# Decays of a Mamba-2 chunk summed in one product each, and two input panels fed from the same k-tile

## The chip, the cores and the metric

The kernel runs on one core of a Trainium2 chip. The metric is the device time of one execution in microseconds (us); the inputs lie in the chip's memory (HBM) when it starts. Five engines work side by side, each through its own list of instructions in order: TensorE (PE in the profile; PEld is its weight loading), VectorE (DVE), ScalarE (ACT), GpSimd (POOL) and SyncE (SP), which here issues the DMA transfers.

## The reference

One decoder layer on 256 tokens of width 1024, all in float32:

```
proj = rms_norm(x) @ w_in            # q, k, v, z, xBC, dt, two gates
y_a  = moba_attention(q, k, v)       # 16 heads; at 256 tokens: causal attention
y_b  = mamba2_mixer(z, xBC, dt)      # conv, chunked scan, gate, grouped norm
x = x + (sigmoid(g_a)*(y_a@Wa) + sigmoid(g_b)*(y_b@Wb)) @ W_out
x = x + swiglu(rms_norm(x))
x = x + (p @ W_pp) * sigmoid(rms_norm(x) @ W_pg)
```

The change touches the scan. With dt = softplus(dt_raw + bias) and a = -dt exp(a_log) for each token and each of 32 heads, in two chunks of 128 tokens:

```
xdt      = xh * dt
decay_in[l, s] = exp(a[s+1] + ... + a[l])   for l >= s, else 0
y_diag   = (C B^T * decay_in) @ xdt
w_end[s] = exp(a[s+1] + ... + a[127]);  states = B^T (xdt * w_end)
y_off    = C @ state of the chunk before, times exp(a[0] + ... + a[l])
```

## The kernel before

Nearly every product is a 512-column *panel*: two PSUM tiles of 128 tokens x 512 columns (`g`, four banks, so two panels at a time), summed over k-tiles of 128 input features. To keep float32 accuracy, weights and activations are split into a high part in the fast float32r format and a low part (`wh`, `wl`, `ah`, `al`), and each k-tile and token half takes three products: ah wh, ah wl, al wh (`Panel.add`, L280). A k-tile is thus six matmuls of 512 columns, a panel of the input projection 48.

Weights come by DMA two k-tiles at a time (512 KB; tag `raw`, four buffers), ScalarE rounds them to `wh` (three buffers) and VectorE subtracts to get `wl` (six buffers) (`load`, L220). The first panel's first half is loaded by single k-tiles, each k-tile of x (128 KB, `load_x`) beside its weights (256 KB); all vectors of constants (`vecs`, 121 KB, with the norm gain of x in columns 0 to 7) come in one transfer behind the first x tile. `split_h` (L262) scales a k-tile of x by the gain and splits it.

The panels stand in a list (L34): six of xBC first (group 4, then 0, 5, 1, 2, 3), then k, q, z and so on. Behind each panel an evacuation (`evac_*`) reads its PSUM; that of xBC multiplies by `rstd1`, which `x_stats` (L311) makes from a second copy of x (`xk`, two transfers of 512 KB). All smaller work (dt, convolution, scan, attention) is made of Python generators that a `Filler` steps between the matmuls of the panels: `fill.now` adds up the TensorE time of what has been issued, and after each part a generator waits until `fill.now` has grown by an entry of the table `LAG` (ns, L68). This gives the program's order. The framework's planner then orders each engine's list with a timing model of its own, by priority: weights ("w"), evacuations ("ev"), small work ("bg"), main matmuls ("mm"). Main matmuls keep their order among themselves.

The scan: `dt_task` (L336) makes dt and a, and splits a into `a_h` and `a_l`; four small products give the sums for `e0` (w_end of chunk 0) and `e1`. For each unit (group g, half qd: four heads) and each chunk c, `decay_rows` (L538) has GpSimd lay out a_h and a_l as two 128 x 4 x 128 tiles (`rr`, four buffers, first used by x), with entry [s, l] = a[s] where l >= s; `seg` (L576) multiplies each by the strict triangle `gt_r` and adds both in PSUM:

```
mm(pseg, gt_r, rr.pop((g, qd, c, 0)), True, False)
mm(pseg, gt_r, rr.pop((g, qd, c, 1)), False, True)
```

ScalarE takes the exponential, VectorE multiplies by the masked C B^T (`cbm`). `prep` makes `xdt` (times dth = dt/2), `out_` the products with it. There are 8 units, so 16 such pairs. `ssm_out` needs the finished groups: it steps the filler until they are there.

Of the kernel before, what the change touches and what calls it, by code (L numbers as in the profile page):

```python
# [68 lines left out]
    "dt": 8257, "dt.t": 2343, "dt.e": 17162, "dt.end": 5569, "xbc": 3815, "xbc.t": 2321, "xbc.end": 7699,  # L69
    "z": 3815, "z.t": 1286, "z.end": 1943, "qk": 13149, "qk.t": 2429, "qk.end": 663, "v": 2577, "cb": 500,  # L70
    "rows": 3610, "prep": 3559, "seg": 722, "seg.next": 7665, "out": 4912, "out.xdt": 3186, "out.end": 0,
    "off": 5300, "off.end": 0, "finish": 6096, "finish.ones": 9336, "sc": 0, "sc.tr": 3063, "tr": 2317,
    "tr.val": 4578, "val": 3570, "val.end": 7415, "m": 500, "res": 6182, "ff": 5466, "ff.end": 5564,
# [34 lines left out]
def tile_layer(ctx: ExitStack, tc: tile.TileContext, xt, xk, pt, vec, w_dt, w_big, w_dn2, w_pp, out):  # L108
# [19 lines left out]
    def nm(s):  # L128
        uid[0] += 1
        return f"{s}_{uid[0]}"  # L130
# [47 lines left out]
    with prio("w"):  # L178
# [23 lines left out]
        nc.gpsimd.tensor_copy(le_r, m_tmp[:, 2])  # L202
        le_q = const.tile([P, P], F32, name="le_q")
# [7 lines left out]
    v = const.tile([P, V_N], F32, name="vecs")  # L211
    xraw = [sb.tile([P, 2, T], F32, tag="rr", bufs=4, name=nm("xraw")) for _ in range(4)]

    def load_x(k, n):
        nc.sync.dma_start(xraw[k // 2][:, k % 2 : k % 2 + n], xt[:, k : k + n])  # L215

    chunk_no = [0]
    first = []

    def load(src, nk):  # L220

        with prio("w"):
            parts = []
            for k in range(0, nk, 2):
                raw = sb.tile([P, 2, 512], F32, tag="raw", bufs=4, name=nm("raw"))
                wh = sb.tile([P, 2, 512], F32R, tag="wh", bufs=3, name=nm("wh"))
                wl = sb.tile([P, 2, 512], F32R, tag="wl", bufs=6, name=nm("wl"))
                n = 2 if len(first) > 1 else 1
                for j in range(0, 2, n):
                    js = slice(j, j + n)  # L230
                    if not first and k + j:
                        load_x(k + j, 1)
                    nc.sync.dma_start(raw[:, js], src[:, k + j : k + j + n])  # L233
                    if not first and not k + j:
                        load_x(0, 1)
                        nc.sync.dma_start(v, vec)
                    if not first and k + j:
                        split_h(k + j)
                    w_ = act(wh[:, js], raw[:, js])
                    if not first:  # L240
                        tc.keep_in_program_order(w_)
                        if not k + j:
                            split_h(0)
                    nc.vector.tensor_sub(wl[:, js], raw[:, js], wh[:, js].bitcast(F32))  # L244
                parts += [(wh[:, 0], wl[:, 0]), (wh[:, 1], wl[:, 1])]
            first.append(1)
            if len(first) == 1:
                load_x(4, 2)
                load_x(6, 2)
        return parts  # L250
# [11 lines left out]
    def split_h(k):  # L262
        g = v[:, V_G1 + k : V_G1 + k + 1]
        xk_ = xraw[k // 2][:, k % 2]
        tc.keep_in_program_order(act(h_act[k][0], xk_, scale=g))
        stt(h_act[k][1], xk_, g, h_act[k][0].bitcast(F32), op0=ALU.mult, op1=ALU.subtract)

    class Panel:
# [3 lines left out]
        def __init__(self, cut=False):  # L272
            self.ps = [psg.tile([P, 512], F32, tag="g", name=nm("g")) for _ in range(2)]
            self.pieces = [(tt, WHOLE, self.ps[tt]) for tt in range(2)]
            if cut:
                other = pb([512])
                self.pieces[1:] = [(1, HALVES[0], self.ps[1][:, HALVES[0]]), (1, HALVES[1], other[:, HALVES[1]])]
            self.first = True

        def add(self, parts, acts, last):  # L280
            n = len(parts)
            if last:
                runs = [(pc, k) for pc in self.pieces for k in range(n)]
            else:
                runs = [(pc, k + j) for k in range(0, n, 2) for pc in self.pieces for j in range(2)]
            for (tt, c, ps), k in runs:
                ah, al = acts[k]
                wh, wl = parts[k]
                ts = slice(tt * P, tt * P + P)
                with prio("mm"):  # L290
                    mm(ps, ah[:, ts], wh[:, c], self.first and k == 0, False, main=True)
                    mm(ps, ah[:, ts], wl[:, c], False, False, main=True)
                    mm(ps, al[:, ts], wh[:, c], False, last and k == n - 1, main=True)
                fill.step()
            self.first = False
# [6 lines left out]
    parts0 = next_chunk()  # L302
    with prio("w"):
        for k in range(4, 8):
            split_h(k)
# [27 lines left out]
    e1 = const.tile([P, 32], F32, name="e1")  # L333
    done = set()

    def dt_task():  # L336
# [55 lines left out]
        with prio("bg"):  # L392

            pe = pb([2, 32])
            mm(pe[:, 0], gt_r, a_h[:, 0], True, False)
            mm(pe[:, 0], gt_r, a_l[:, 0], False, True)
            mm(pe[:, 1], le_r, a_h[:, 1], True, False)
            mm(pe[:, 1], le_r, a_l[:, 1], False, True)
            act(e0, pe[:, 0], AF.Exp)
            act(e1, pe[:, 1], AF.Exp)  # L400
# [117 lines left out]
    def ssm_task():  # L518
# [57 lines left out]
        def seg(g, qd):  # L576
            for c in range(2):
                with prio("bg"):
                    pseg = pb([4, P])
                    mm(pseg, gt_r, rr.pop((g, qd, c, 0)), True, False)  # L580
                    mm(pseg, gt_r, rr.pop((g, qd, c, 1)), False, True)
# [210 lines left out]
    for n, (kind, i, _) in enumerate(PANELS):  # L792
        if kind == "yb":
            ssm_out(i)
            continue
        pan = Panel()
        for hf in range(2):
            pan.add(parts0 if n == hf == 0 else next_chunk(), h_act[4 * hf : 4 * hf + 4], last=hf == 1)
            if n == 0 and hf == 1:
                x_stats()  # L800
            if n == hf == 0:
                fill.spawn(dt_task(), 0)
        gen = evac[kind](kind, i, pan)
        t = next(gen)
        fill.spawn(gen, 0, t - fill.now)
# [219 lines left out]
```

## Time and profile before

| | us |
|---|---|
| median of 3 runs | 614.92 (614.15 to 614.96) |
| the profiled execution, own time | 614.88 |
| its span in the trace | 613.2 |
| PE busy | 604.2 (99%) |
| VectorE busy | 441.8 (72%) |
| ScalarE busy | 341.5 (56%) |
| GpSimd busy | 60.4 (10%) |
| DMA queue of SyncE | 103.29 MB, 51.8% of 16 DMA engines |

Times in the trace count from the span's start. A matmul's duration is longer than the distance to the next one, because matmuls are pipelined; costs of TensorE are therefore read as distances between starts. A note in square brackets is idle time of that engine before the row, and what ended it.

### The profile page before, as it was taken

The page shows a single profiled execution, that of the slowest core. Times are in us where ns is not written, and L with a number is a line of the kernel's source. Part 1 is how long each engine was busy: PE and PEld are TensorE (multiplying, and loading weights), DVE is VectorE, ACT ScalarE, POOL GpSimd, SP SyncE. Part 2 cuts the span into 40 slices and gives each one's busy share as a digit, 9 for nine tenths or more (in the row PEclk, how much of TensorE's full clock was granted, in tenths as well). Part 3 has the DMA queues.
Part 4 walks back from the last instruction along what each step waited for, and adds up shares of the span by engine and source line. Part 5 has one row for each costly group of instructions (what it writes and reads, how often), then busy time and mean ns, then how long its engine had stood idle before and what let it go on. Part 6 is the DMA issues. An engine that isn't in the chain of part 4 may idle for free.

```text
span 613.2 us, 8146 instructions
## 1 busy us (share of the span) xinstructions
PE 604.2 (99%) x2964; PEld 494.0 (81%) x2964; DVE 441.8 (72%) x712; ACT 341.5 (56%) x522; POOL 60.4 (10%) x61
## 2 busy tenths in 40 slices
PE   7999999999999999999999999999999999999997
PEld 5888888877777878888788888888888888888886
DVE  4489899978898775768897576656676666645465
ACT  5568566646584445568467544656554454435353
POOL 1001206623122200200000000000000000000000
PEclk9999999999999999999999999999999999999999
DMA  8845544344324545554444467555556556565541
GB/s 254 310 160 179 173 149 156 125 161 139 103 93 134 181 142 176 169 178 156 131 155 153 144 190 236 175 183 188 189 165 202 183 171 207 172 196 183 192 151 68
DMA packets 30793, 103.81 MB, mean 169 GB/s; under 512 B 3361, under 2 KB 4385, under 8 KB 30753
## 3 DMA queue, kind: packets, MB, share of 16 engines
q1 hardware_dynamic: 30752, 103.29, 51.8%
q8 instruction: 23, 0.38, 0.2%
q14 instruction: 18, 0.14, 0.1%
HBM read 102.23 MB, written 1.05 MB: 168 GB/s over the span
## 4 chain that ended last, share of the span: by engine, by line
PE 92%; DVE 3%; DMA 1%; POOL 1%; SPq 1%; issue 1%; ACT 0%; POOLq 0%
PE g L164 80%; PE pb L164 7%; PE pb L174 5%; DMA raw<-in_w_big 1%; POOL tiny L479 1%; DVE wl L244 1%; DVE s L428 0%; SPq L215 0%; DVE s L480 0%; DVE tiny L476 0%; SPq L233 0%; DVE s L584 0%; DVE tiny L477 0%; DVE s L604 0%; DVE s L491 0%
## 5 line engine op out<-in xcount | busy, mean ns | idle before, releaser
L164 PE MATMUL g<-wh,s 128*128 128x512 f32 x1504 | 484.8, 394 | 2.7 <-DVE s L480 1.3
L164 PEld LDWEIGHTS g<-wh,s 128*128 128x128 f32 x1504 | 281.6, 188 | 62.1 <-issue 2.7
L244 DVE TENSOR_TENSOR wl<-raw,wh 128x1024 fp32r<-128x1024 f32 (+1 forms) x192 | 231.4, 1208 | 120.8 <-ACT wh L148 118.0
L148 ACT ACTIVATE wh<-raw 128x1024 fp32r<-128x1024 f32 (+1 forms) x192 | 199.8, 1043 | 174.2 <-PE g L164 142.4
L164 PE MATMUL g<-wl,s 128*128 128x512 f32 x752 | 295.1, 392 | 0.7 <-DVE wl L244 0.7
L164 PEld LDWEIGHTS g<-wl,s 128*128 128x128 f32 x752 | 141.5, 188 | 30.0 <-DVE wl L244 2.5
L148 ACT ACTIVATE s<-pb 128x512 f32<-128x512 f32 (+5 forms) x76 | 36.8, 506 | 30.9 <-PE pb L174 18.7
L174 PE MATMUL pb<-ident,s 128*128 128x128 f32 (+1 forms) x302 | 46.9, 273 | 0.0
L174 PEld LDWEIGHTS pb<-ident,s 128*128 128x128 f32 (+1 forms) x302 | 37.3, 140 | 10.7 <-issue 0.9
L164 PE MATMUL pb<-s,s 128*64 128x128 f32 (+7 forms) x312 | 40.1, 303 | 0.0
L148 ACT ACTIVATE s<-g,rstd 128x512 f32<-128x512 f32 (+2 forms) x50 | 28.5, 583 | 19.2 <-PE g L164 18.9
L164 PEld LDWEIGHTS pb<-s,s 128*64 128x64 f32 (+3 forms) x312 | 30.9, 163 | 9.4 <-issue 5.2
L148 ACT ACTIVATE s<-pb,vecs 128x256 f32<-128x256 f32 (+2 forms) x48 | 25.5, 552 | 18.1 <-PE pb L174 11.4
L300 POOL TENSOR_TENSOR rstd<-tiny,mhalf 128x2 f32<-128x2 f32 x3 | 2.1, 706 | 323.9 <-DVE tiny L299 297.6
L428 DVE SCALAR_TENSOR_TENSOR s<-pb,vecs,s 128x255 f32<-128x255 f32 (+2 forms) x72 | 31.5, 472 | 0.3 <-ACT s L148 0.2
L545 POOL TENSOR_SCALAR_AFFINE_SELECT rr<-a_h 128x512 fp32r<-128x512 f32 x16 | 17.9, 1117 | 104.4 <-PE pb L164 75.9
L148 ACT ACTIVATE s<-s 128x512 f32<-128x512 f32 (+3 forms) x24 | 19.1, 794 | 9.1 <-DVE s L873 4.0
L479 POOL TENSOR_TENSOR tiny<-tiny,mhalf 128x8 f32<-128x8 f32 x8 | 15.9, 1993 | 56.0 <-DVE tiny L477 56.0
L545 POOL TENSOR_SCALAR_AFFINE_SELECT rr<-a_l 128x512 fp32r<-128x512 f32 x16 | 19.5, 1221 | 0.0
L148 ACT ACTIVATE s<-s,tiny 128x128 f32<-128x128 f32 (+1 forms) x32 | 14.1, 445 | 6.3 <-DVE tiny L698 6.3
L917 DVE SCALAR_TENSOR_TENSOR s<-g,rstd,s 128x256 f32<-128x256 f32 x22 | 10.6, 481 | 7.4 <-ACT s L148 7.4
L584 DVE TENSOR_TENSOR s<-s,s 128x512 f32<-128x512 f32 x16 | 13.2, 832 | 0.1
(114 smaller groups left out, 268.0 us busy)
## 6 DMA issues: line engine op xcount, KB each, us to landing
raw<-in_w_big SPq DMA_DIRECT2D x180, 512.0 KB, 4.0
raw<-in_w_big SPq DMA_DIRECT2D x8, 256.0 KB, 6.0
s<-in_xk SPq DMA_DIRECT2D x4, 512.0 KB, 6.6
raw<-in_w_pp SPq DMA_DIRECT2D x2, 512.0 KB, 3.2
raw<-in_w_dn SPq DMA_DIRECT2D x2, 512.0 KB, 4.2
out<-s SPq DMA_DIRECT2D x3, 256.0 KB, 2.0
xraw<-in_xt SPq DMA_DIRECT2D x4, 128.0 KB, 3.6
xraw<-in_xt SPq DMA_DIRECT2D x2, 256.0 KB, 6.5
```

What stands on the lines that cost most here:

```text
L148: return nc.scalar.activation(o, i, f, **kw)
L164: queue(nc.tensor.matmul(o, lhsT, rhs, start=start, stop=stop).ins, main)
L174: queue(nc.tensor.transpose(o, i, ident[: i.shape[0], : i.shape[0]]).ins, False)
L244: nc.vector.tensor_sub(wl[:, js], raw[:, js], wh[:, js].bitcast(F32))
L300: nc.gpsimd.tensor_tensor(dst, t, mhalf[:, : ss.shape[-1]], op=ALU.pow)
L428: stt(cc[:, sft:], pu[:, j, : T - sft], cw[3 - sft], cc[:, sft:], op0=ALU.mult, op1=ALU.add)
L479: nc.gpsimd.tensor_tensor(f, ms, mhalf, op=ALU.pow)
L545: nc.gpsimd.affine_select(r, bcast(part[:, c, h0 : h0 + 4].bitcast(F32), P), pattern=[[0, 4], [1, P]], compare_op=ALU.is_ge, fill=0.0, bas ...
L584: nc.vector.tensor_tensor(m, m, cbm[:, g, c].unsqueeze(1).to_broadcast([P, 4, P]), op=ALU.mult)
L917: stt(t[:, tt], pan.ps[tt][:, :T], r, t[:, tt], op0=ALU.mult, op1=ALU.mult)
```

## The change

Three edits and a new `LAG` table.

**Decays.** a_h stays in `rr`, a_l does not. One product gives the low part's sums S(s) of all heads and both chunks (`pe[:, 0:2]`), clamped to 80 either way; dth is multiplied by exp(S), so x dt carries exp(S(s)). The factor exp(-S(l)) that is then too many comes back through rows: -S(l) is transposed and split (`low_h`, `low_l`), and two small DMAs for each unit and chunk put it into the two rows of `rr` that were free. Row 0 meets a row of ones in `gt1_r` (a copy of the triangle with row 0 filled), row 127 is free for l < 127.

```
     pe = pb([4, 32])
     mm(pe[:, 0:2], gt_r, a_l, True, True)
     mm(pe[:, 2], gt_r, a_h[:, 0], True, True)
     mm(pe[:, 3], le_r, a_h[:, 1], True, False)
     mm(pe[:, 3], le_r, a_l[:, 1], False, True)
     nc.vector.tensor_scalar(low, pe[:, 0:2], -80.0, 80.0, op0=ALU.max, op1=ALU.min)
...
     act(el, low, AF.Exp)
     act(e0, pe[:, 2], AF.Exp)
     act(e1, pe[:, 3], AF.Exp)
     nc.vector.tensor_mul(dth, dth, el)
     yield fill.now + LAG["dt.low"]
     transpose(plow[:64], low.rearrange("p c h -> p (c h)"))
     act(low_h[:64], plow[:64], scale=-1.0)
     stt(low_l[:64], plow[:64], -1.0, low_h[:64].bitcast(F32), op0=ALU.mult, op1=ALU.subtract)
...
-                for n, part in enumerate((a_h, a_l)):
...
+                    bcast(a_h[:, c, h0 : h0 + 4].bitcast(F32), P), pattern=[[0, 4], [1, P]],
...
+    rows = slice(32 * c + h0, 32 * c + h0 + 4)
+    nc.sync.dma_start(r[0:1].bitcast(F32), low_h[rows].bitcast(F32))
+    nc.sync.dma_start(r[P - 1 : P, :, : P - 1].bitcast(F32), low_l[rows, : P - 1].bitcast(F32))
...
-    mm(pseg, gt_r, rr.pop((g, qd, c, 0)), True, False)
-    mm(pseg, gt_r, rr.pop((g, qd, c, 1)), False, True)
+    mm(pseg, gt1_r, rr.pop((g, qd, c)), True, True)
```

**The first two panels.** `load_first` loads the weights of both; ScalarE's queue issues the gains alone (`g1`, 128 x 8) and x's k-tile 0, SyncE the rest: for k-tiles 0 to 3 x, panel 0's weights, panel 1's weights, then `vecs`, then the same by pairs.

```
for k in (0, 2):
    tiles = [w_tiles() for _ in range(2)]
    for j in range(2):
        if k + j:
            load_x(k + j, 1)
        for b in range(2):
            nc.sync.dma_start(tiles[b][0][:, j], w_big[2 * b][:, k + j])
    for j in range(2):
        split_h(k + j)
        for b in range(2):
            tc.keep_in_program_order(split_w(tiles[b], slice(j, j + 1)))
```

The matmuls follow: k-tile 0 for both panels, then 1, 2, 3; then the pair 4, 5 for panel 0, for panel 1; then 6, 7 for panel 0 with its evacuation, and for panel 1 with its own. `dt_task` and `x_stats` start before k-tile 4 (before: behind the first half and the end of the first panel).

**LAG.** Most entries are new, among them `dt.e` 17162 to 24762, `z` 3815 to 8310, `out` 4912 to 9793, `m` 500 to 5271, `ff` 5466 to 232, `finish.ones` 9336 to 2544; `dt.low` is added.

## Rows read from the trace of the kernel before

**Rows 1.** The page: busy time by engine, and the span in 40 slices (busy tenths of PE, and the granted clock of TensorE in tenths of full speed).

```profile
PE 604.2 (99%) x2964; PEld 494.0 (81%) x2964; DVE 441.8 (72%) x712; ACT 341.5 (56%) x522; POOL 60.4 (10%) x61
...
PE   7999999999999999999999999999999999999997
...
PEclk9999999999999999999999999999999999999999
```

**Rows 2.** All waits of TensorE: what it waited for, us in total, times, longest.

```profile
PE g L164 <- DVE s L480: 1.3, 1, 1.3
PE pb L187 <- DVE ones L191: 1.1, 1, 1.1
PE g L164 <- ACT wh L148: 1.0, 2, 0.6
PE g L164 <- DVE wl L244: 0.7, 3, 0.2
PE g L164 <- ACT s L148: 0.5, 1, 0.5
```

**Rows 3.** Panel matmuls alone (tile g) in three stretches: length, then busy us and count of PE, PEld, DVE, ACT, then the clock, the DMA engines' busy share, GB/s.

```profile
5.80:14.30 8.50, 7.01 (x24) 4.19 (x24) 0.00 (x0) 0.00 (x0) 1.00 0.97 294
14.30:15.04 0.74, 0.51 (x1) 0.19 (x1) 0.00 (x0) 0.00 (x0) 1.00 1.02 412
15.04:24.50 9.46, 9.44 (x41) 7.50 (x41) 0.00 (x0) 0.00 (x0) 1.00 0.89 291
```

**Rows 4.** The chain of waits, stretches of TensorE alone: start, us, matmuls; the last two are a pair of decay products and four transposes.

```profile
228.96 10.94 PE g L164 x48
...
242.86 19.07 PE g L164 x84
...
97.30 0.47 PE pb L164 x2
97.77 0.44 PE pb L174 x4
```

**Rows 5.** The timeline of the start: start, us, engine, line, operation.

```profile
0.78 1.28 ACT L148 ACT_TABLE_LOAD   x1 [0.78 <-PEq L1014]
...
1.23 0.42 SPq L215 DMA_DIRECT2D xraw<-in_xt  x1
...
4.37 0.63 ACT L148 ACTIVATE wh<-raw 128x512 fp32r<-128x512 f32 x1 [2.09 <-DMA raw<-in_w_big]
...
5.30 0.91 ACT L148 ACTIVATE s<-xraw,vecs 128x256 fp32r<-128x256 f32 x2 [0.31 <-DMA vecs<-in_vec]
...
5.87 0.50 PE L164 MATMUL g<-wh,s 128*128 128x512 f32 x1 [0.52 <-ACT s L148]
...
7.87 0.48 DVE L266 SCALAR_TENSOR_TENSOR s<-xraw,vecs,s 128x256 fp32r<-128x256 f32 x1
...
9.23 0.63 ACT L148 ACTIVATE wh<-raw 128x512 fp32r<-128x512 f32 x1 [1.61 <-DMA raw<-in_w_big]
...
9.90 0.69 DVE L244 TENSOR_TENSOR wl<-raw,wh 128x512 fp32r<-128x512 f32 x1 [1.55 <-ACT wh L148]
...
14.34 0.51 PE L164 MATMUL g<-wh,s 128*128 128x512 f32 x1 [0.57 <-ACT wh L148]
...
15.06 0.50 PE L164 MATMUL g<-wl,s 128*128 128x512 f32 x1 [0.22 <-DVE wl L244]
```

**Rows 6.** The page: DMA issues, KB each, median us from issue to landing.

```profile
raw<-in_w_big SPq DMA_DIRECT2D x180, 512.0 KB, 4.0
...
xraw<-in_xt SPq DMA_DIRECT2D x4, 128.0 KB, 3.6
...
out<-s SPq DMA_DIRECT2D x2, 128.0 KB, 1.9
```

**Rows 7.** The timeline from 19 to 34 us: the second xk transfer, dt's 16 products, the squares of x, rstd1, the first evacuation, the third panel's first matmul.

```profile
19.65 0.55 SPq L316 DMA_DIRECT2D s<-in_xk  x1
...
24.53 2.03 PE L164 MATMUL pb<-s,s 128*64 128x256 f32 x16
...
28.21 0.63 ACT L148 ACTIVATE s<-s 128x512 f32<-128x512 f32 x1 [2.55 <-DMA s<-in_xk]
...
30.79 1.27 ACT L148 ACTIVATE s<-g,rstd 128x512 f32<-128x512 f32 x2 [0.29 <-POOL rstd L300]
...
33.26 0.47 PE L164 MATMUL g<-wh,s 128*128 128x512 f32 x1
```

**Rows 8.** All engines in three stretches: length, then busy us (count) of PE, PEld, DVE, ACT, POOL, the clock, DMA share, GB/s.

```profile
40.00:100.00 60.00, 60.00 (x292) 50.20 (x291) 55.97 (x110) 39.71 (x59) 11.26 (x8) 1.00 0.50 160
100.00:130.00 30.00, 28.72 (x155) 22.75 (x154) 28.82 (x45) 17.13 (x24) 18.19 (x13) 1.00 0.48 150
...
200.00:600.00 400.00, 400.00 (x1920) 329.36 (x1919) 267.69 (x389) 212.36 (x312) 10.30 (x8) 1.00 0.54 175
```

**Rows 9.** Around the rows of the decays: two VectorE products of L584, the GpSimd instruction that runs beside the second, and SyncE's waits between 60 and 200 us (total, times, longest).

```profile
94.79 0.67 DVE L584 TENSOR_TENSOR s<-s,s 128x512 f32<-128x512 f32 x1
...
98.79 1.62 POOL L545 TENSOR_SCALAR_AFFINE_SELECT rr<-a_l 128x512 fp32r<-128x512 f32 x1
...
99.83 1.12 DVE L584 TENSOR_TENSOR s<-s,s 128x512 f32<-128x512 f32 x1
...
SPq L233 <- DVE wl L244: 108.3, 32, 6.8
```

More of the change, by code (lines that the diff above doesn't have):

```diff
@@ L68 @@
 LAG = {
[L69 to L73, printed above, removed]
+    "dt": 9538, "dt.t": 3583, "dt.e": 24762, "dt.low": 1745, "dt.end": 5569, "xbc": 3815, "xbc.t": 1612,
+    "xbc.end": 7699, "z": 8310, "z.t": 1286, "z.end": 1974, "qk": 14749, "qk.t": 2429, "qk.end": 663,
+    "v": 3190, "cb": 436, "rows": 3738, "prep": 3559, "seg": 921, "seg.next": 7841, "out": 9793,
+    "out.xdt": 3087, "out.end": 0, "off": 4613, "off.end": 0, "finish": 6096, "finish.ones": 2544, "sc": 857,
+    "sc.tr": 2402, "tr": 822, "tr.val": 5876, "val": 3318, "val.end": 8813, "m": 5271, "res": 4539, "ff": 232,
+    "ff.end": 5364,
 }
@@ L211, in tile_layer, with load_x, w_tiles, split_w @@
     v = const.tile([P, V_N], F32, name="vecs")
+    g1 = const.tile([P, 8], F32, name="g1")
     xraw = [sb.tile([P, 2, T], F32, tag="rr", bufs=4, name=nm("xraw")) for _ in range(4)]
[L214 to L218, printed above, removed]
+    def load_x(k, n, queue=nc.sync):
+        queue.dma_start(xraw[k // 2][:, k % 2 : k % 2 + n], xt[:, k : k + n])
+    chunk_no = [4]
+    def w_tiles():
+        return (sb.tile([P, 2, 512], F32, tag="raw", bufs=4, name=nm("raw")),
+                sb.tile([P, 2, 512], F32R, tag="wh", bufs=3, name=nm("wh")),
+                sb.tile([P, 2, 512], F32R, tag="wl", bufs=6, name=nm("wl")))
+    def split_w(tiles, js=slice(0, 2)):
+        raw, wh, wl = (t[:, js] for t in tiles)
+        rounded = act(wh, raw)
+        nc.vector.tensor_sub(wl, raw, wh.bitcast(F32))
+        return rounded
+    def parts_of(tiles):
+        return [(tiles[1][:, j], tiles[2][:, j]) for j in range(2)]
     def load(src, nk):
@@ L224, in load @@
             for k in range(0, nk, 2):
[L225 to L231, printed above, removed]
-                        load_x(k + j, 1)
[L233 to L244, printed above, removed]
@@ L262, in split_h @@
     def split_h(k):
-        g = v[:, V_G1 + k : V_G1 + k + 1]
+        g = g1[:, k : k + 1]
         xk_ = xraw[k // 2][:, k % 2]
@@ L285, in add, with step @@
                 runs = [(pc, k + j) for k in range(0, n, 2) for pc in self.pieces for j in range(2)]
[L286 to L295, printed above, removed]
+            for pc, k in runs:
+                self.step(pc, parts[k], acts[k], last and k == n - 1)
+        def step(self, piece, part, act_, last):
+            tt, c, ps = piece
+            ah, al = act_
+            wh, wl = part
+            ts = slice(tt * P, tt * P + P)
+            begun = id(piece) in self.begun
+            self.begun.add(id(piece))
+            with prio("mm"):
+                mm(ps, ah[:, ts], wh[:, c], not begun, False, main=True)
+                mm(ps, ah[:, ts], wl[:, c], False, False, main=True)
+                mm(ps, al[:, ts], wh[:, c], False, last, main=True)
+            fill.step()
     def rstd_of(dst, ss, scale, eps=EPS):
@@ L300, in rstd_of @@
         nc.gpsimd.tensor_tensor(dst, t, mhalf[:, : ss.shape[-1]], op=ALU.pow)
[L302 to L305, printed above, removed]
+    parts0 = load_first()
     rstd1 = const.tile([P, 2], F32, name="rstd1")
@@ L790, in ssm_out, with evacuate @@
                         stt(acc[:, tt], pan.ps[tt], r, acc[:, tt], op0=ALU.mult, op1=ALU.add)
-    for n, (kind, i, _) in enumerate(PANELS):
+    def evacuate(kind, i, pan):
+        gen = evac[kind](kind, i, pan)
+        t = next(gen)
+        fill.spawn(gen, 0, t - fill.now)
+    pans = [Panel() for _ in range(2)]
+    for k in range(0, 8, 2):
+        if k == 4:
+            fill.spawn(dt_task(), 0)
+            x_stats()
+        for ks, bs in ([((k,), (0, 1)), ((k + 1,), (0, 1))] if k < 4 else [((k, k + 1), (0,)), ((k, k + 1), (1,))]):
+            for b in bs:
+                for pc in pans[b].pieces:
+                    for kk in ks:
+                        pans[b].step(pc, parts0[b][kk], h_act[kk], kk == 7)
+                if k == 6:
+                    evacuate(*PANELS[b][:2], pans[b])
+    for kind, i, _ in PANELS[2:]:
         if kind == "yb":
@@ L797, in tile_layer @@
         for hf in range(2):
[L798 to L805, printed above, removed]
+            pan.add(next_chunk(), h_act[4 * hf : 4 * hf + 4], last=hf == 1)
+        evacuate(kind, i, pan)
     def split_t(toks, scale_cols, const_scale, acts, delay):
```

68 lines of the change are left out of this document (46 added, 22 removed).

## The prediction

> **What bounds the kernel now.** I read the page first: TensorE is busy 99% of the span at the full clock, and only the first of the 40 slices falls below nine tenths apart from the last [rows 1]. The list of all its waits is short: 4.6 us, of which one wait of 1.3 us is in mid-kernel and 1.1 us is the wait for the warm-up's operand; the rest is in the start [rows 2]. So time can come from two places: fewer matmuls, or a start in which TensorE is fed.
>
> The start is worse than the wait list says, because a waiting TensorE still shows its last, pipelined matmul as busy. A fed panel takes 10.94 us for 48 matmuls, 0.228 each; a longer stretch gives 19.07 / 84 = 0.227 [rows 4]. From the first panel matmul at 5.87 [rows 5] to dt's first product at 24.53 [rows 7] there are 24 + 1 + 41 = 66 matmuls [rows 3]. Fed, they need 66 x 0.228 = 15.05 us; they took 18.66. Lost: 3.6 us, all but some tenths before 15.06.
>
> Why is it lost? In this stretch the DMA engines are busy 97% at 294 GB/s [rows 3]. One k-tile asks for 128 + 256 KB in six matmuls (1.37 us): 287 GB/s, with nothing to spare, and the 121 KB of `vecs` go ahead of the second x tile. ScalarE waits 1.61 us for weights before 9.23 [rows 5]. The start is bound by transfers.
>
> Behind the start VectorE is nearly full: 55.97 of 60 us from 40 to 100 and 28.82 of 30 from 100 to 130, against 268 of 400 later [rows 8]. The 1.3 us wait falls there: TensorE is short of full only from 100 to 130, by 1.28 us. TensorE still sets the time, but VectorE has only (60 - 55.97) + (30 - 28.82) = 5.2 us left in these 90 us.
>
> **Part 1, one decay product in place of two.** 16 matmuls of 512 columns go. A pair takes 0.47 us [rows 4], so one is 0.235: 16 x 0.235 = -3.76 us. TensorE has no gap there to swallow it: its only wait in mid-kernel lies before 130 us [rows 2, 8]. Bounds: about five of the 16 fall before 130 us, beside the nearly full VectorE, and might bring nothing, so -2.6; at best a switch between kinds of matmul goes with them, but the remaining product is still switched to and from, so -3.8. I take -3.76.
>
> Added on TensorE: one transpose, 0.11 by the four in 0.44 us [rows 4], and a low-part product of 64 columns in place of one of 32. Call it +0.15, between 0 and 0.25. VectorE gets a clamp, a product and a split, each narrower than the 512-wide row of 0.69 us [rows 5], so 0 to 2 us in all; they lie in the dt chain, which must finish before the first unit and has the C B^T products before it anyway. ScalarE has 44% idle [rows 1] for its two instructions. GpSimd loses 16 instructions like that of 1.62 us [rows 9].
>
> One gain hides here. A VectorE product of the decays took 0.67 us alone and 1.12 us beside GpSimd's layout instruction [rows 9]; half of these layouts go, so up to 16 x 0.45 = 7.2 us of VectorE come free, part of it before 130 us. The page "SBUF — State Buffer" of the Trainium skill (section "SBUF: two separate sides") says why: GpSimd and a VectorE instruction with two SBUF inputs take one port pair in turns, exclusively, and the loser blocks. By that rule the 1.3 us wait at 128 us could vanish, and this row agrees with it. By the trace alone I book nothing, since the wait hung on the power on GpSimd and on the evacuation, which stay.
>
> **Part 2, rows by DMA.** 32 small transfers are put in SyncE's queue, each behind a layout on GpSimd, and ahead of weights. Transfer time: the nearest rows are 1.9 us (128 KB out) and 4.0 us (512 KB of weights, behind others) from issue to landing [rows 6]. Issue costs 0.42 us of SyncE each [rows 5], 13 us in all, in an engine that mostly waits. The new wait is on SyncE: a row transfer holds what stands behind it until GpSimd is done (about 1.6 us [rows 9]); behind it stand weight loads, which have four raw and three rounded buffers, each good for 12 matmuls = 2.7 us, so a hold of 2 us should not reach TensorE. The other way round is worse: a row transfer behind a weight load that waits for a free buffer (108.3 / 32 = 3.4 us on average [rows 9]). One pass is 1.6 + 3.4 + 4.0 = 9.0 us. What gives room is that `rr` now holds two units instead of one, so layout and rows can run a unit ahead. Bounds 0 to +10 us; I take +0.5.
>
> **Part 3, the start.** With a shared k-tile, 128 + 512 KB feed 12 matmuls (2.74 us): 239 GB/s against 294 measured. ScalarE needs 0.46 + 2 x 0.63 = 1.7 us for it, VectorE 0.48 + 2 x 0.69 = 1.9 [rows 5]: both below 2.74. So TensorE becomes the bound as soon as the first tiles are there. New waits in this order: the first low part comes 0.69 us behind the first high part, as at 14.34 to 15.06 now (0.72 instead of 0.23: 0.5 lost [rows 5]); and the second split of k-tile 2 waits for a buffer that panel 0's k-tile 1 frees, a tile earlier than it is used. I leave 0.9 us of the 3.6 lost: -2.7, between -3.4 and -1.
>
> The first matmul: now scaling by the gain waits for `vecs` until 5.30 [rows 5]. If gains and x tile are there with the first weights at 4.37, 0.46 + 0.63 us lead to about 5.5: -0.4. Bounds: they land earlier and only 0.63 is left after 4.37, -0.8; or ScalarE issues them only after its table load and the warm-up, from about 2.3, twice 0.42 and 3.6 us to landing [rows 5, 6], so at 6.7, then 1.1 more: +1.9. I take -0.4, since the two issues wait for nothing.
>
> What is late next: the third panel needs banks that only an evacuation frees, and that needs `rstd1`. Now the second xk transfer, issued at 19.65, lands at 28.21, the evacuation starts at 30.79, and the third panel comes at 33.26 [rows 7], with the second panel in hand as cover. After the change panels 0 and 1 end almost together: 5.5 + 0.9 + 96 x 0.228 = 28.3, plus dt's products (1.87 us, if put there) 30.2. The first evacuated bank takes 0.64 us, so `rstd1` may come at about 29.5 without loss; at today's 30.79 the loss is 1.2 to 3.1. The last weights of the pair (5.2 MB in all) and xk share one saturated queue. The statistics start after as many matmuls as before (48), which now end earlier. I take +0.5, between 0 and +3.
>
> **Part 4, LAG.** The entries move small work among the main matmuls. Its matmuls stay; after 130 us there is no wait to win. To lose: a product placed before its operand stops the queue. To win before: at most the 1.3 us. I take 0, between -1.3 and +2.
>
> **Sum.** -3.76 + 0.15 + 0.5 - 2.7 - 0.4 + 0.5 + 0 = -5.7. From the profiled execution's own 614.88 (span 613.2 and 1.7 around it; median of the runs 614.92) that is 609.2; I say 609.3.
>
> **Rivals.**
> *The start's gain is absorbed* (late `rstd1`, or VectorE's full stretch, which has 5.2 us idle to give for 3.1 + 1.2 us of earlier demand). For it: the late `rstd1` and the little idle time of VectorE [rows 7, 8]. Against it: its idle time is mostly waiting for TensorE's progress and shrinks by itself. What stays is 11 products behind 130 us and a little of the rest: -2.6 - 0.5, so 611.8, from 611.2 to 613.6.
> *Everything lands.* Port time freed, no late rows, wait gone: -3.76 + 0.15 - 3.4 - 0.6 - 1.3 = -8.9, so 606.0; from 605.5 to 607.5.
> *Rows late.* The rows come after their product's place in TensorE's fixed list, behind weight loads blocked on buffers. One pass of 9.0 us must fit into the time between a unit's layout and its product; where it meets a second blocked load it is 12.4. If layouts run a unit ahead (about 10 us), the lateness is up to 2.4 us; at 1.5 us for each of 8 units 12 us come on, less the 6.2 gained otherwise: 620.7. It decides the sign from 0.8 us a unit. For it: SyncE waits 108 of 140 us [rows 9]. Against it: the longer lead with half the tiles.
> *No effect* (the products go, but the lists' new order costs as much): 613.7 to 616.1.
>
> **How the numbers follow.** Forecast 607.5 to 611.2: 0.52. Everything lands: 0.14. Absorbed: 0.17. No effect: 0.07. Slower, rows late above all: 0.10. Within 0.2%, about 1.2 us, a measurement cannot tell the kernels apart. Faster 0.83, same 0.07, slower 0.10. The range 606.0 to 613.5 leaves out the last two cases and the ends of the second and third.
>
> **What would show it.** Right: 16 decay products at line seg, no pairs; first panel matmul near 5.5 and 96 panel matmuls done by about 30; TensorE's waits at the start near 1 us. Wrong: a wait of TensorE on a DMA into `rr`, or on the evacuation of the first panel near 28 us; a first matmul after 7; a longer wait near 125 us on VectorE. A time above 613.5 would mean that a queue, not TensorE, sets the scan.

## The result and the profile after

The changed kernel takes 611.33 us (median of 4 runs, 610.74 to 612.0) against 614.56 before on the same chip (614.15 to 614.96): ratio 0.9948, 95% interval 0.9931 to 0.9965, or 3.2 us less (half a per cent). The forecast was 609.3. The profiled execution took 612.0, its span 610.2.

The page of the changed kernel, lines as in [rows 1]; 15 of TensorE's matmuls are gone and a third of GpSimd's time:

```profile
PE 601.2 (99%) x2949; PEld 493.1 (81%) x2949; DVE 437.8 (72%) x715; ACT 341.9 (56%) x524; POOL 40.2 (7%) x47
...
PE   7999999999999999999999999999999999999997
...
PEclk9999999999999999999999999999999999999999
```

All waits of its TensorE, to be held against [rows 2]:

```profile
PE g L165 <- ACT wh L149: 2.9, 1, 2.9
PE pb L188 <- DVE ones L192: 1.1, 1, 1.1
PE pb L165 <- DVE s L474: 0.6, 1, 0.6
```

Five rows became three. The many short waits of the start are one of 2.9 us, and the wait in mid-kernel is 0.6 instead of 1.3. Where the 2.9 us lie, and what follows them, the timeline shows (start, us, engine, line, operation; lines as in [rows 5, 7]):

```profile
0.79 0.41 ACTq L254 DMA_DIRECT2D g<-in_vec  x1
...
1.29 0.40 ACTq L221 DMA_DIRECT2D xraw<-in_xt  x1
...
7.13 0.51 ACT L149 ACTIVATE s<-xraw,g 128x256 fp32r<-128x256 f32 x1 [4.40 <-DMA xraw<-in_xt]
...
8.21 0.80 PE L165 MATMUL g<-wh,s 128*128 128x512 f32 x1 [2.86 <-ACT wh L149]
...
9.53 1.05 PE L165 MATMUL g<-wh,s 128*128 128x512 f32 x2
10.38 0.63 PE L165 MATMUL g<-wl,s 128*128 128x512 f32 x1
10.81 1.05 PE L165 MATMUL g<-wh,s 128*128 128x512 f32 x2
...
31.84 0.67 ACT L149 ACTIVATE s<-g,rstd 128x512 f32<-128x512 f32 x1
...
33.05 2.04 PE L165 MATMUL pb<-s,s 128*64 128x256 f32 x16
34.93 0.40 PE L165 MATMUL g<-wh,s 128*128 128x512 f32 x1
```

x's first k-tile is issued at 1.29 and is usable at 7.1; the first panel matmul comes at 8.21, not at 5.87 as before, and not at the forecast 5.5. Then read the distances between starts: two matmuls from 9.53 to 10.38 and one from there to 10.81 are 0.43 us each, against 0.227 in [rows 4]. 512 columns in 0.43 us is TensorE's lower level of 1.2 GHz. Only near 14 do the steps become 0.227. The third panel still starts right behind dt's products, but at 34.93 against 33.26: the start lost 1.7 us, where by the sum it should have gained 2.6.

So the whole gain, and 1.7 us more, comes after 35 us: 33.26 to the span's end 613.2 was 579.9 us, 34.93 to 610.2 is 575.3, or 4.7 less. 3.6 of it are the 16 products less the added matmuls, 0.65 the shorter wait; 0.4 are left over. By stretch, as in [rows 8]:

```profile
40.00:100.00 60.00, 60.00 (x294) 49.82 (x293) 56.55 (x118) 39.41 (x60) 4.50 (x6) 1.00 0.49 154
100.00:130.00 30.00, 29.39 (x156) 22.90 (x155) 28.86 (x47) 18.86 (x28) 12.72 (x9) 1.00 0.50 154
...
200.00:600.00 400.00, 400.00 (x1921) 329.67 (x1920) 267.45 (x389) 214.25 (x314) 11.85 (x8) 1.00 0.54 173
```

VectorE is as full as before (56.55 and 28.86 us), though its decay products got shorter. Last, around the rows of the decays (first the lines of the page: busy us, mean ns; then waits of SyncE's queue), as in [rows 9]:

```profile
L632 DVE TENSOR_TENSOR s<-s,s 128x512 f32<-128x512 f32 x16 | 11.5, 722 | 0.0
```

```profile
SPq L595 <- POOL rr L591: 28.1, 8, 5.7
```

SyncE stood 28.1 us at the row transfers, waiting for GpSimd's layouts, and no wait of TensorE hangs on it.

### The profile page after: what moved, and what is told of

The parts are those of the page before. It is cut to its first block, busy times and chain, and to the rows that moved or that the text cites. A ratio compares the mean times of both kernels' runs of the same rounds, so it can differ in the third digit from the quotient of the medians.

```text
span 610.2 us, 8184 instructions
## 1 busy us (share of the span) xinstructions
PE 601.2 (99%) x2949; PEld 493.1 (81%) x2949; DVE 437.8 (72%) x715; ACT 341.9 (56%) x524; POOL 40.2 (7%) x47
## 4 chain that ended last, share of the span: by engine, by line
PE 97%; DMA 1%; DVE 1%; ACT 0%; issue 0%; ACTq 0%
PE g L165 84%; PE pb L165 7%; PE pb L175 5%; DMA xraw<-in_xt 1%; DVE s L474 0%; ACT wh L149 0%; DVE wl L233 0%; ACT s L149 0%; DVE s L526 0%; DVE tiny L522 0%; DVE s L1019 0%; DVE s L1020 0%; ACTq L254 0%; DVE tiny L523 0%; ACT L149 0%
## 5 line engine op out<-in xcount | busy, mean ns | idle before, releaser
L175 PEld LDWEIGHTS pb<-ident,s 128*128 128x128 f32 x302 | 37.8, 140 | 11.5 <-issue 1.2
L175 PE MATMUL pb<-ident,s 128*128 128x128 f32 x302 | 46.7, 272 | 0.0
L149 ACT ACTIVATE s<-g,rstd 128x512 f32<-128x512 f32 (+2 forms) x50 | 28.5, 583 | 22.4 <-PE g L165 21.8
L149 ACT ACTIVATE s<-pb,vecs 128x256 f32<-128x256 f32 (+2 forms) x48 | 26.0, 552 | 11.8 <-PE pb L175 7.4
L591 POOL TENSOR_SCALAR_AFFINE_SELECT rr<-a_h 128x512 fp32r<-128x512 f32 x16 | 14.3, 902 | 104.3 <-PE pb L165 66.8
L525 POOL TENSOR_TENSOR tiny<-tiny,mhalf 128x8 f32<-128x8 f32 x8 | 15.7, 1966 | 61.1 <-ACT s L149 31.5
L978 DVE SCALAR_TENSOR_TENSOR s<-g,rstd,s 128x256 f32<-128x256 f32 x22 | 10.6, 481 | 7.4 <-ACT s L149 7.3
L632 DVE TENSOR_TENSOR s<-s,s 128x512 f32<-128x512 f32 x16 | 11.5, 722 | 0.0
L979 DVE SCALAR_TENSOR_TENSOR s<-g,rstd,s 128x256 f32<-128x256 f32 x22 | 10.6, 484 | 0.8
```

Source lines behind the costliest of these rows:

```text
L149: return nc.scalar.activation(o, i, f, **kw)
L175: queue(nc.tensor.transpose(o, i, ident[: i.shape[0], : i.shape[0]]).ins, False)
L525: nc.gpsimd.tensor_tensor(f, ms, mhalf, op=ALU.pow)
L591: nc.gpsimd.affine_select(r, bcast(a_h[:, c, h0 : h0 + 4].bitcast(F32), P), pattern=[[0, 4], [1, P]], compare_op=ALU.is_ge, fill=0.0, base ...
L632: nc.vector.tensor_tensor(m, m, cbm[:, g, c].unsqueeze(1).to_broadcast([P, 4, P]), op=ALU.mult)
L978: stt(t[:, tt], pan.ps[tt][:, :T], r, t[:, tt], op0=ALU.mult, op1=ALU.mult)
```

## The experiments on the start

Three things could explain the lost start: x's tile is slow on ScalarE's queue, the tile and the gains disturb each other, or TensorE's lower level is the larger part. All five kernels here are the changed kernel with one edit.

**x's first tile by SyncE.**

```
-            load_x(0, 1, nc.scalar)
+            load_x(0, 1)
```

> The changed kernel, with x's k-tile 0 issued by SyncE ahead of all weights; the gains (g1) stay on ScalarE's queue. Theory A (x came late only because of ScalarE's queue): the tile lands by about 4.5 us instead of 7.04, the first panel matmul starts near 5.6 instead of 8.21, no matmul runs at the half clock, the third panel starts near 30 instead of 34.93, and the time is 611.3 - 5 = about 606.5 us. Theory B (the transfers of two panels' weights are simply too many at once): the tile is not much earlier, first matmul after 7, time 610.5 to 611.5 us.

Measured: 608.05 us (607.27 to 608.82), ratio 0.989 [0.9877, 0.9903], 3.3 us better than the change itself. Its timeline:

```profile
3.49 0.51 ACT L149 ACTIVATE s<-xraw,g 128x256 fp32r<-128x256 f32 x1 [0.76 <-DMA g<-in_vec]
...
30.51 0.40 PE L165 MATMUL g<-wh,s 128*128 128x512 f32 x1
```

The tile is there at 3.5 in place of 7.1, the first panel matmul comes at 5.22, steps that wait for no operand take 0.23, and the third panel starts at 30.51, 4.4 us earlier than in the changed kernel and 2.75 earlier than before. This is the start that the prediction's sum describes. Theory A holds, but the time came 1.5 us above what it expected: 0.6 of that is that the start gave back 4.4 us, not 5. Behind the third panel the two traces are equal (575.3 and 575.4 us), and the two profiled executions do differ by 4.4 us (612.0 and 607.61); the rest lies in the spread of the runs. Fed all the while, 96 panel matmuls and dt's products (21.8 + 1.9 us) would have ended at 28.9; 1.6 us are still lost, since ScalarE waits for weights before 6.38 and 8.21 (1.2 and 0.8 us).

**The gains by SyncE instead, x alone on ScalarE's queue.**

```
-            nc.scalar.dma_start(g1, vec[:, V_G1 : V_G1 + 8])
+            nc.sync.dma_start(g1, vec[:, V_G1 : V_G1 + 8])
```

> The changed kernel, with x's k-tile 0 alone on ScalarE's queue and the gains first on SyncE's. Theory E (whatever comes second on ScalarE's queue lands 4.7 to 5.8 us after its issue, the first 2.7 to 3.7): x now lands by 4.5 us, first panel matmul 5.2 to 5.9, no half clock, time 607.5 to 608.5 us as with x on SyncE. Rival F (a tile of x is late on ScalarE's queue in any place): x lands after 6, first matmul after 7, time 610 us or more.

Measured: 608.42 us (607.2 to 609.44), ratio 0.9894 [0.9881, 0.9908], the same as the kernel above within the runs' spread, and as theory E had it:

```profile
3.50 0.51 ACT L149 ACTIVATE s<-xraw,g 128x256 fp32r<-128x256 f32 x1 [0.78 <-DMA xraw<-in_xt]
```

So the tile is not slow because ScalarE issues it. It was slow with the gains ahead of it on that queue; alone there it is also issued half a microsecond earlier, at 0.79, ahead of SyncE's first weights (1.24).

**The two exchanged: x first, the gains second.**

```
-            nc.scalar.dma_start(g1, vec[:, V_G1 : V_G1 + 8])
             load_x(0, 1, nc.scalar)
+            nc.scalar.dma_start(g1, vec[:, V_G1 : V_G1 + 8])
```

> The changed kernel, with the two transfers of ScalarE's queue exchanged: x's k-tile 0 first, then the gains. Theory A1 (the gains' 128 small pieces ahead of x hold it): x lands by 4.5 to 5 us, first matmul at 5.6 to 6.2, time about 606.5 to 607.5 us. Theory A2 (what ScalarE's queue sends is served behind SyncE's backlog, whatever its size): whichever of the two is second lands near 7, the first matmul stays near 8, time 610.5 to 611.5 us.

Measured: 609.98 us (609.77 to 610.95), ratio 0.9924 [0.9912, 0.9936].

```profile
1.29 0.40 ACTq L255 DMA_DIRECT2D g<-in_vec  x1
...
6.03 0.51 ACT L149 ACTIVATE s<-xraw,g 128x256 fp32r<-128x256 f32 x1 [3.31 <-DMA g<-in_vec]
```

Time and first matmul (7.11) lie between the two cases. Now the gains, 4 KB, come last: issued at 1.29, usable at 6.0. So size isn't what makes the second late: it lands 4.7 (gains) to 5.75 us (x) after its issue, while either of them, alone on that queue, is usable after 2.7.

The DMA view shows what the two have in common: each counts 144 packets on ScalarE's queue (q10), whether they hold 4 KB or 128. Where both queues have work, they move packets at nearly one pace. In the changed kernel, from 3.0 to 3.5 us (packets, MB, share of 16 DMA engines):

```profile
q1 hardware_dynamic: 63, 0.12, 65.0%
q10 hardware_dynamic: 60, 0.01, 13.1%
```

On ScalarE's queue the count reaches 144 near 3.7 us; most of the tile's packets come behind that, the last before 7.0, beside SyncE's weights (q1), the first of which were issued at 0.80. By this the second is late because 144 packets of its own queue and as many of the weights go ahead of it. That is argued from the counts: no run kept the order on ScalarE's queue and took the weights away.

**Longer warm-up.**

```
-        for _ in range(9):
+        for _ in range(15):
```

> The changed kernel, with 15 warm-up products instead of 9, so that TensorE works until about 8.2 us, when its first operand comes. Theory (of the 5 us lost at the start about half is the clock, which fell while TensorE stood still from 5.35 to 8.21): first panel matmul still near 8.2, but 0.23 instead of 0.43 us from one to the next, all 96 done 2.8 us earlier, time about 608.5 us. Rival (the matmuls of 8 to 14 us are paced by their operands, not by the clock): the distances stay, time 611 us.

Measured: 609.47 us (609.2 to 612.12), ratio 0.992 [0.9907, 0.9933]. x is as late as in the changed kernel, but TensorE stands still for 1.0 us, not 2.9:

```profile
8.07 0.49 PE L165 MATMUL g<-wh,s 128*128 128x512 f32 x1 [1.01 <-ACT wh L149]
8.79 0.50 PE L165 MATMUL g<-wl,s 128*128 128x512 f32 x1 [0.23 <-DVE wl L233]
9.13 0.63 PE L165 MATMUL g<-wh,s 128*128 128x512 f32 x2
9.59 0.39 PE L165 MATMUL g<-wl,s 128*128 128x512 f32 x1
```

The two matmuls from 9.13 to 9.59 are 0.23 us apart: the upper level. The operands come as before, so they don't pace the 0.43 us steps of the changed kernel. The third panel comes at 32.33, 2.6 us earlier than there, with a first matmul only 0.14 us earlier. So about 2.5 us of the start's loss are TensorE's lower level behind the gap, and the lateness itself some 2 us. The profiled executions differ by as much (612.0 and 609.45); the medians differ by 1.9, and one of the six runs took 612.12.

**Panel 0's first weights on ScalarE's queue, x and gains by SyncE.**

```
-            nc.scalar.dma_start(g1, vec[:, V_G1 : V_G1 + 8])
-            load_x(0, 1, nc.scalar)
+            nc.sync.dma_start(g1, vec[:, V_G1 : V_G1 + 8])
+            load_x(0, 1)
...
-                        nc.sync.dma_start(tiles[b][0][:, j], w_big[2 * b][:, k + j])
+                        queue = nc.sync if k + j + b else nc.scalar
+                        queue.dma_start(tiles[b][0][:, j], w_big[2 * b][:, k + j])
```

> The changed kernel with other queues for the first transfers: panel 0's weights of k-tile 0 alone on ScalarE's queue; the gains and x's k-tile 0 first and second on SyncE's. If what is first on ScalarE's queue lands promptly whatever its size (2.7 us after issue for 128 KB), the weights, which now are the last operand, come at 3.6 to 4.0 in place of 4.5, the first panel matmul at 4.7 to 5.1 in place of 5.2, and the time is 607.4 to 608.1, against 608.05 and 608.4 with x or the gains moved. If even a first transfer of 256 KB on that queue is slow, its weights land after 5, the first matmul comes after 6, and the time is above 609.

Measured: 608.64 us (607.55 to 609.16), ratio 0.989 [0.9874, 0.9907]: between the two cases, and no better than the first run.

```profile
1.24 0.42 SPq L221 DMA_DIRECT2D xraw<-in_xt  x1
...
4.80 0.51 ACT L149 ACTIVATE s<-xraw,g 128x256 fp32r<-128x256 f32 x1 [2.08 <-DMA xraw<-in_xt]
5.22 0.61 ACT L149 ACTIVATE wh<-raw 128x512 fp32r<-128x512 f32 x1
```

ScalarE waited for x, this time second on SyncE's queue (3.5 us from issue), and the first matmul came at 5.89, the third panel at 32.07. The weights were there when ScalarE turned to them. When they landed the DMA view tells: the last of the 144 packets on ScalarE's queue moves before 4.1 us, 3.3 us after the issue. So a first transfer of 256 KB is prompt there too; what moved back was x.

## The experiments on the parts

The change has three parts that can be built alone: start, LAG, decays. With before and after, six more kernels make all eight combinations, each of them compared with before on its own chip (614.56 to 614.94). No mixed kernel was given a table of its own: the two tables are those of before and after, so a row shows a part beside a table that came with another kernel.

| start | LAG | decays | us | |
|---|---|---|---|---|
| old | old | old | 614.6 to 614.9 | before |
| old | old | new | 626.29 | decays alone |
| old | new | old | 617.63 | LAG alone |
| old | new | new | 616.65 | LAG and decays |
| new | old | old | 632.08 | start alone |
| new | old | new | 623.12 | no LAG |
| new | new | old | 616.37 | no decays |
| new | new | new | 611.33 | after |

**Decays alone** (the hunks of the decays, and the new entry; the tables else those of before).

```
-    "dt": 8257, "dt.t": 2343, "dt.e": 17162, "dt.end": 5569, "xbc": 3815, "xbc.t": 2321, "xbc.end": 7699,
+    "dt": 8257, "dt.t": 2343, "dt.e": 17162, "dt.low": 1745, "dt.end": 5569, "xbc": 3815, "xbc.t": 2321, "xbc.end": 7699,
...
-                    mm(pseg, gt_r, rr.pop((g, qd, c, 0)), True, False)
-                    mm(pseg, gt_r, rr.pop((g, qd, c, 1)), False, True)
+                    mm(pseg, gt1_r, rr.pop((g, qd, c)), True, True)
```

> The kernel before with the decay edit alone: one product instead of two, rows by DMA, the low part in x dt; the start and the LAG table of before, with dt.low 1745 added. Theory (16 products of 0.235 us go, rows are hidden): 614.6 - 3.8 + 0.15 = about 610.9 us, no wait of TensorE at the decay products. Rival 1 (the new LAG table brought the gain behind the start): 613 to 615 us. Rival 2 (rows late without the new table): above 615, with waits of TensorE on transfers into rr.

Measured: 626.29 us (625.77 to 626.44), ratio 1.0184 [1.0171, 1.0197]; far off. Its waits of TensorE:

```profile
PE pb L164 <- DVE s L446: 3.7, 1, 3.7
PE g L164 <- DVE s L498: 2.6, 1, 2.6
PE g L164 <- ACT s L148: 2.0, 2, 1.3
PE pb L164 <- ACT s L148: 1.8, 1, 1.8
```

and two stretches (columns as in [rows 8]):

```profile
60.00:80.00 20.00, 20.00 (x100) 16.73 (x99) 14.61 (x24) 10.18 (x16) 6.51 (x4) 1.00 0.56 186
...
110.00:120.00 10.00, 6.26 (x35) 4.61 (x34) 8.68 (x18) 4.00 (x6) 4.80 (x4) 0.91 0.46 152
```

No wait for a DMA into `rr` is among them. VectorE does 14.61 us of work between 60 and 80 us, where it did 18.22 before; it waits 4.4 us there for weights that ScalarE rounds, against 1.4 before. The work left undone is missing later: the convolution (L446) and the scaling of q and k (L498) come when TensorE already stands at their products. All waits of TensorE here add up to 14.3 us, 9.7 more than before, while the time, without the products' 3.6, is 15.1 above before. For the other 5.4 there is the granted clock, which falls behind the waits (0.91 in this row); its mean of 0.993 over 624.7 us would make 4.4 us, an estimate that takes TensorE as fed all the while.

**The same without the 32 row transfers** (the decays then lack the factor exp(-S(l)), and GpSimd's layouts are not completed).

```
-                    nc.sync.dma_start(r[0:1].bitcast(F32), low_h[rows].bitcast(F32))
-                    nc.sync.dma_start(r[P - 1 : P, :, : P - 1].bitcast(F32), low_l[rows, : P - 1].bitcast(F32))
```

> The kernel with the decay edit alone and the old table (626.3 us), leaving out the 32 row transfers, so that the decays lack the low part's factor exp(-S(l)). Rival D (the row transfers in SyncE's queue cost the 11.5 us): about 611 us, no waits of TensorE before 140 us. Theory C (the old table's order of VectorE's work costs them): 620 to 627 us, VectorE idle for some us between 60 and 80 and TensorE waiting on it later.

Measured: 627.18 us (625.66 to 627.97), ratio 1.0196 [1.018, 1.0211]. The same waits stand:

```profile
PE pb L164 <- DVE s L446: 3.7, 1, 3.7
PE g L164 <- DVE s L498: 2.6, 1, 2.6
```

The transfers cost nothing that can be seen. What is left is the order in which the old table puts the work; that VectorE's list is where it hurts is read from the waits.

**LAG alone, and LAG with the decays.** The first is before with the new table:

```
-    "z": 3815, "z.t": 1286, "z.end": 1943, "qk": 13149, "qk.t": 2429, "qk.end": 663, "v": 2577, "cb": 500,
...
+    "xbc.end": 7699, "z": 8310, "z.t": 1286, "z.end": 1974, "qk": 14749, "qk.t": 2429, "qk.end": 663,
```

> The kernel before with the new LAG table alone (its entry dt.low is not used). Theory C (the table places VectorE's work between 30 and 130 us so that the new kernel does not stall; the old kernel did not stall there either): nothing to win but the 1.3 us wait, 613 to 616 us. Rival (the table is better for any kernel): 612 us or less. Third way (the table fits only the new kernel): over 618 us, with waits of TensorE on VectorE before 140 us.

Measured: 617.63 us (616.58 to 618.68), ratio 1.0045 [1.0032, 1.0058]: between the two cases. The second has the hunks of the decays beside that table:

```
-                    mm(pseg, gt_r, rr.pop((g, qd, c, 0)), True, False)
-                    mm(pseg, gt_r, rr.pop((g, qd, c, 1)), False, True)
+                    mm(pseg, gt1_r, rr.pop((g, qd, c)), True, True)
```

> The kernel before with the decay edit and the new LAG table, but the start of before. Theory C (the 626.3 us of the decay edit alone are the old table's doing, not the row transfers'): 614.7 - 3.8 + 0.15, and the wait before 130 us shorter by up to 1.3: 609.7 to 611.5 us. Rival D (the decay edit with the old start stalls with any table, because the row transfers come late): 615 us or more.

Measured: 616.65 us (615.36 to 617.28), ratio 1.0027 [1.0017, 1.0038]. Theory C missed, and the time lies in rival D's bracket, but not for D's reason: the one decay product among its longer waits (at 117.01, for 1.9 us) waits 1.6 us at 117.06 with LAG alone as well, where no rows are transferred. Both lose a third of TensorE's time in the same 10 us (first LAG alone, then with the decays):

```profile
110.00:120.00 10.00, 6.61 (x44) 4.16 (x40) 8.49 (x16) 5.91 (x10) 5.73 (x5) 1.00 0.49 157
```

```profile
110.00:120.00 10.00, 6.13 (x42) 3.78 (x40) 8.56 (x16) 5.83 (x10) 4.85 (x4) 1.00 0.55 158
```

After these four, one theory was left: the table fits only the start with which it came. The other three combinations put that to the test.

**The change without its decays.** The old pairs, new start and new table:

```
-                    mm(pseg, gt1_r, rr.pop((g, qd, c)), True, True)
+                    mm(pseg, gt_r, rr.pop((g, qd, c, 0)), True, False)
+                    mm(pseg, gt_r, rr.pop((g, qd, c, 1)), False, True)
```

> The change without its decay edit: the new start and the new LAG table stay, the decays are the pairs of before (a_h and a_l, two products each). Sums theory: each part keeps its own worth, so the 16 products and what VectorE and GpSimd save come back and nothing else: 611.3 + 3.8 - 0.15 = 615.0, and TensorE's waits stay those of the changed kernel (4.6 us in all). Fit theory: the table was good only for the whole; with the old decays the order of VectorE's full stretch from 35 to 140 us changes and TensorE waits there for tiles s of VectorE, 2 us or more in all: 616.5 to 622. In either case the start is that of the changed kernel: third panel near 34.9.

Measured: 616.37 us (614.99 to 616.64), ratio 1.0017 [1.0007, 1.0027], at the border of the two theories. The only wait in mid-kernel is

```profile
PE g L165 <- DVE s L688: 0.7, 1, 0.7
```

so this fits the sums: no new stall, and the decays are worth 5.0 us where start and table are the new ones. 3.6 of them are the products less what is added; the other 1.4 are not traced to a row (the runs of each of the two kernels spread over 1.3 to 1.7 us; behind the third panel the two traces differ by 4.9). Decay products of VectorE (L612) take 791 ns in the mean with 32 layouts, 722 with 16.

**The change without its LAG.** New start, new decays, the old table with `dt.low`:

```
-    "xbc.end": 7699, "z": 8310, "z.t": 1286, "z.end": 1974, "qk": 14749, "qk.t": 2429, "qk.end": 663,
...
+    "z": 3815, "z.t": 1286, "z.end": 1943, "qk": 13149, "qk.t": 2429, "qk.end": 663, "v": 2577, "cb": 500,
...
```

> The change without its new LAG table: new start and new decays stay, LAG is that of before with the one entry dt.low added. Sums theory: the table was put at 0 in the prediction, so 611.3, from 610.5 to 613. Fit theory: the old table with the new decays cost 15 us of waits for VectorE's tiles with the old start; with the new start, in which panels 0 and 1 end together and dt starts at another place, it costs again, 3 us or more: 614.5 to 626, with waits on s of VectorE between 80 and 190 us.

Measured: 623.12 us (621.59 to 624.66), ratio 1.0135 [1.0113, 1.0156]. The fit theory holds: the table, booked at nothing, is worth 11.8 us where the other two parts are there. Its waits, and the stretch of the longest:

```profile
PE pb L164 <- DVE s L473: 3.7, 1, 3.7
PE g L164 <- ACT wh L148: 3.0, 1, 3.0
PE pb L164 <- ACT s L148: 2.2, 2, 1.9
```

```profile
110.00:120.00 10.00, 6.26 (x30) 4.61 (x30) 8.71 (x16) 4.94 (x8) 6.25 (x4) 1.00 0.50 171
120.00:130.00 10.00, 10.00 (x58) 7.89 (x56) 8.84 (x14) 5.58 (x8) 1.22 (x2) 0.83 0.27 97
```

**The start alone.** Before with `load_first` and the shared k-tiles:

```
+    parts0 = load_first()
...
+            for b in bs:
+                for pc in pans[b].pieces:
+                    for kk in ks:
+                        pans[b].step(pc, parts0[b][kk], h_act[kk], kk == 7)
```

> The kernel before with the new start alone (its table and its decays stay). Sums theory: the third panel comes at about 34.9 in place of 33.3, as in the changed kernel, and nothing else changes: 614.8 + 1.7 = 616.5, from 615.8 to 617.2. Fit theory: the old table was fitted to the old start; the xBC evacuations now come in pairs and VectorE's order changes, TensorE waits 2 us or more before 140 us: 618 to 625.

Measured: 632.08 us (632.05 to 632.55), ratio 1.0282 [1.0267, 1.0297], worse than the fit theory had it. Its third panel comes at 34.28, so only a microsecond is lost in the start itself; the rest are waits, and behind them the granted clock (0.83 from 130 to 140 us, 0.93 from 140 to 200). The longest two waits, and what VectorE, GpSimd and TensorE did before the second of them:

```profile
PE g L164 <- DVE s L687: 4.0, 1, 4.0
PE pb L174 <- DVE s L507: 3.1, 1, 3.1
```

```profile
132.15 0.68 DVE L503 TENSOR_REDUCE tiny<-s 128x8 f32<-128x512 f32 x1
...
132.86 0.23 DVE L504 TENSOR_SCALAR tiny<-tiny,eps 128x8 f32<-128x8 f32 x1
133.17 1.64 POOL L506 TENSOR_TENSOR tiny<-tiny,mhalf 128x8 f32<-128x8 f32 x1 [4.58 <-DVE tiny L504]
...
134.84 0.69 DVE L507 TENSOR_TENSOR s<-g,tiny 128x512 f32<-128x512 f32 x1 [0.71 <-POOL tiny L506]
...
135.68 0.63 PE L174 MATMUL pb<-ident,s 128*128 128x128 f32 x4 [3.05 <-DVE s L507]
```

This is how a misfit looks: the norm of q or k is a chain from VectorE to GpSimd and back, 135.53 - 132.15 = 3.4 us long; it began only when TensorE's list had nearly come to the transposes that read it, because other work stood ahead of it on VectorE (its input, a square by ScalarE, was there at 130.30). TensorE waits out the rest of the chain.

## Why the prediction was right and wrong

The time fell in the range, 2 us above the forecast. That it came so near is partly luck: the start missed by 4.3 us against (-2.6 in the sum, +1.7 measured), the rest by 1.6 for (-3.1 and -4.7).

- *Part 1, 16 products, -3.76, adds +0.15.* Right. In the changed kernel a product takes 0.23 to 0.24 us of the chain. Taken back alone the edit is worth 5.0 us; 3.6 are these. The bound that five of the 16 might bring nothing beside a full VectorE didn't show.
- *Port time, booked at nothing.* Right in size. The page "SBUF — State Buffer" of the Trainium skill (section "SBUF: two separate sides") agrees in direction: with half of the layouts the products fall from 832 to 722 ns, 16 x 0.11 = 1.7 us of VectorE (from 791 with the same start and table, 1.1 us), not the up to 7.2 that one pair of rows suggested.
- *Part 2, rows, +0.5.* Nothing can be seen: issuing one took 0.57 us, not 0.42, and SyncE waits 28.1 us for GpSimd, but TensorE not at all; without the 32 transfers (old start and table) the longest waits stayed as they were. The rival of late rows has fallen. Layouts do run ahead: the first rows are issued at 80.84, the first product that reads them comes at 94.8.
- *Part 3, sharing k-tiles, -2.7.* The direction is right, as the kernel with x by SyncE shows: first matmul 5.22 (0.65 earlier than before, where the sum had 0.4), third panel 2.75 earlier. So sharing brought 2.1 there, and 1.6 us stay lost instead of the 0.9 allowed: TensorE isn't the bound as soon as the first tiles are there, since the weights still come late for some microseconds. In the change itself this gain was hidden.
- *First matmul -0.4, because "the two issues wait for nothing".* This step failed. They didn't wait to be issued (0.79 and 1.29), but the second landed 5.75 us after its issue, where the row that was taken had 3.6 [rows 6]: +2.3 in place of -0.4. The page of the kernel before also lists 6.0 us for its eight first weight loads of 256 KB and 6.5 for its x pairs, so late landings in the start were there to be read. The upper bound of +1.9 came from another cause. And the prediction had no term for what a still TensorE does to its own clock: about 2.5 us.
- *rstd1 late, +0.5.* Nothing: the third panel follows dt's products without a gap, also where they end at 30.5 (x by SyncE).
- *Part 4, LAG, 0, from -1.3 to +2.* The second step that failed. Alone it is +2.7; with the other two parts -11.8; with the start alone -15.7 (632.08 to 616.37); with the decays alone -9.6 (626.29 to 616.65). The term was priced as if the other parts left VectorE's order alone. They don't: start and decays without the table come to 623.1, above before.
- *The rival "absorbed".* Its bracket (611.2 to 613.6) holds the time, its mechanism not: `rstd1` isn't late and VectorE has no more to give back than before. The gain was lost ahead of the first matmul.

1.4 us of the decays' 5.0 are not traced to a row.

## What to carry to other kernels

Where one engine is nearly full beside the bound one, the parts of a change may not add up: here a new order of its list cost more than the instructions saved. So build the parts alone, and count a table of delays as part of each edit; a part that looks bad beside another kernel's table may be good with its own, which no run here tried. Look up, for the very first transfers, what stands ahead on the same queue, and count its packets, not its bytes: taking 4 KB away from ahead of 128 KB brought 2.9 us here, where 16 products of 512 columns bring 3.8. And a gap before the first matmuls can be paid twice, once as a wait and once in TensorE's steps behind it.

## What was not expected of the hardware

- The second transfer on ScalarE's queue landed 4.7 us (4 KB) to 5.75 us (128 KB) after issue, with SyncE's weights beside it; either of them alone on that queue was usable after 2.7, and a first one of 256 KB landed in 3.3. The page "DMA: Bandwidth & Descriptors" of the Trainium skill (section "Issuing engines are not separate DMA queues") has it that transfers of all engines run on the same 16 DMA engines and interleave, and that issuing from several saves only the time of issuing. The packets do interleave here (63 to 60 in half a microsecond). Where x stood mattered all the same, 3.6 us at the landing and 3.3 us in the time; since moving it changed its place in the order too, this is no test of the issuing engine alone.
- After 2.86 us without a matmul TensorE's steps were 0.43 us for 512 columns (1.2 GHz) until near 14; with the longer warm-up, after 1.01 us, they were 0.23. The page "TensorE: Matmul & The Clock Gate" of the Trainium skill (section "What's actually happening") tells of a clock gate with these two levels, set by how busy the engine has been; the traces agree with the levels. In the changed kernel the granted clock reads 1.00 all through this stretch, so that column doesn't show it and the distances between starts do; in the kernel without its LAG, whose start is the same, it shows both (columns as in [rows 8], steps of 0.43 there too):

```profile
9.00:10.00 1.00, 0.93 (x2) 0.83 (x3) 1.00 (x4) 1.00 (x3) 0.00 (x0) 0.50 1.10 338
```

- Which gap brings the lower level is not shown. With LAG alone, on the old start, gaps of 0.73 and 0.85 us were followed by the same 0.43 us steps and a clock of 0.50 from 9 to 11 us, while the kernel before has gaps of 0.52 and 0.39 there and keeps 0.23. Behind waits in mid-kernel the column fell to 0.83 without the new LAG.
- The eight combinations lie between 611.3 and 632.1 us, with TensorE's instructions the same but for the 16 products and one small transpose.
